# Query-block pipeline of both heads, and a top-k search in two alternating groups, in a two-layer decoder trunk

## The chip, the cores and the metric

The kernel runs on 1 core of a Trainium2 chip. The metric is device microseconds for one execution; the time of a kernel is the median of its runs. Engines are called PE (TensorE), DVE (VectorE), ACT (ScalarE), POOL (GpSimd) and SP (the engine whose queue issues the DMAs).

## What is computed

The reference is a trunk of two post-norm layers on x of 1024 tokens by 1024 features, float32. Each layer projects x once and feeds four groups of four heads; the group outputs are multiplied by a SiLU gate, projected back, added to x and normalised.

```python
def hybrid_layer(x, ...):
    p = split_columns(einsum("bsd,de->bse", x, w_in))
    ...
    for i in range(S // 128):                 # 8 query blocks, keys up to the block's end
        o_a = stick_breaking_block(...)       # sigmoid logits, reverse cumulative sum over keys
        o_b = diff_block(...)                 # two softmax maps, p0 - lam * p1, RMS norm per head
        o_c = dsa_block(...)                  # softmax over the 256 keys with the highest index scores
        o_d = mla_block(...)                  # low-rank attention with a rotary part
    y = concatenate(outs) * silu(p["gate"])
    return layer_norm(ALPHA * x + y @ w_out, ln_g, ln_b)
```

The index scores of group C are a weighted sum over 8 small heads of relu(q k); `top_k` takes 256 keys of each query.

## The kernel before, in words

**Work units.** A layer is walked in ten units (`ORDER`, line 42): s0 and s1 compute the index scores (`g_scores`), then a0, a1, d0, d1, b0, b1, c0, c1 are the attention groups, each unit two heads (`softmax_pair`, line 385). A unit goes over eight query blocks i; block i has n = 128(i+1) keys.

**Background.** Projections of the layer (`proj`, line 227: 24 matmuls of 512 columns into one bank, for two halves of the tokens), the low-rank chains of group D (`g_dkw` line 682, `g_dqw` line 718) and, from b1 on, half of the output projection (`g_out`, line 789) are generators in one list (`BGSEQ`). Each unit yields weights w, and `back.run(quota * w)` (line 1116) lets that much background be written between the unit's own steps. The order written is a priority: the instructions of each engine are put in their final order when the program is built, so in the trace the background stands between the attention's pieces, also where the program text has it elsewhere. Two calls shift that: `tc.high_priority(n)` and `tc.keep_in_program_order(ins)`.

**Steps of an attention unit** (`push`, line 363; loop at 498). For block i: stage 1 computes the scores of both heads into PSUM and the weights in SBUF; stage 2, once per head, transposes the weights by PE (`transposed`, line 344, line 95 in the trace: matmuls into a bank `trp`, then an ACT copy to `PT`, line 356); stage 3 multiplies by v (`pv`) and, every fourth block, calls `finalize` (line 323). `push` is called for each head: scores(i), background, transposes of (i-1, head 1), background, pv(i-1), transposes of (i, head 0), scores(i+1) and so on.

**Group A** (`stick`, line 392): each head's scores z take a buffer of their own of two PSUM banks (`sc`, 2 buffers). Four ACT operations (lines 403 to 406), a DVE scan (407), a DVE subtraction that reads z for the last time (408), and an ACT exponential (409). Groups B, C, D (`on_rows`, line 412): chunks of 512 keys; DVE copies each out with a running minimum (lines 436 and 438), ACT takes the exponential (442). Group B combines its two maps with line 465.

**PSUM.** `mm` has two banks, for projections; `tr` has one, `pv` one, `sc` two buffers of two banks. A transposed group of four blocks goes to `tr`, except in b0, b1, c0, c1 from the fifth key block on, where it goes to `mm` (line 349). SBUF tiles of the weights, of PT and of most background results share one pool of 8 (`wrk`, `N_P`).

**Top-k** (`g_topk`, line 855) is a generator of 24 steps, all on DVE: two counts over the six blocks 7 to 2, a maximum, 11 halvings of a threshold, three steps that find the eight largest values below the threshold (`below`, lines 911 to 914), six masks (`mask`, lines 946 to 951; the first with a few small operations and `ps_fail`), and a conditional that closes the search. A halving is

```python
counts(SB, t, cnt)          # six counting operations, line 874
nc.vector.scalar_tensor_tensor(neg, cnt, NSEL - 4.5, mx, op0=ALU.is_gt, op1=ALU.mult)
nc.vector.tensor_scalar(mx, mx, 0.5, None, op0=ALU.mult)
nc.vector.tensor_tensor(lo, lo, neg, op=ALU.add)
nc.vector.tensor_tensor(t, lo, mx, op=ALU.add)
```

The first count of each halving is kept in program order. `with_topk` (line 1072) pulls steps as a unit advances: 8 over a0, 10 over a1, 4 over d0, the rest in d1.

Of the kernel before, what the change touches and what calls it, by code (L numbers as in the profile page):

```python
# [41 lines left out]
ORDER = [('s0', 37.2, 0, 0.6), ('s1', 38.4, 0, 0.65), ('a0', 47.1, 8, 0.65), ('a1', 63.6, 10, 0.7), ('d0', 30.7, 4, 0.65), ('d1', 24.9, 4, 0.65), ('b0', 55.1, 0, 0.65), ('b1', 68.8, 0, 0.65), ('c0', 43.6, 0, 0.65), ('c1', 0.0, 0, 0.7)]  # L42
LNP = 1
TR_MM, PT_DVE = ('b0', 'b1', 'c0', 'c1'), ()
OUT_DVE = 1
PIN_A, PIN_S = 2, 0
OUT_AT = ('b1', 0.3)
FRAC, W0, W1 = 1, 2, 0.5
# [29 lines left out]


class Paced:  # L80


    def __init__(self, tc):
        self.tc, self.pin = tc, False

    def _issue(self, ins):
        if self.pin:
            self.tc.keep_in_program_order(ins)
        self.pin = False

    def matmul(self, *a, **k):
        self._issue(self.tc.nc.tensor.matmul(*a, **k))  # L92

    def transpose(self, *a, **k):
        self._issue(self.tc.nc.tensor.transpose(*a, **k))  # L95
# [3 lines left out]
def trunk(ctx: ExitStack, tc: tile.TileContext, t: dict, out: bass.AP, depth=DEPTH, dbg=None):  # L99
# [223 lines left out]
    def finalize(g, et, c, pv, gs, rl, subv):  # L323
        if g != 1:
            nc.vector.tensor_tensor(gs, pv, gs, op=ALU.mult)
            if g > 1:
                nc.vector.tensor_tensor(gs, rl, gs, op=ALU.mult)
        else:
            o = half("o_h")
            nc.scalar.activation(o, pv, AF.Copy)  # L330
            nc.vector.tensor_tensor(o, rl, o, op=ALU.mult)
            sq = half("sq_h")
            nc.scalar.activation(sq, o, AF.Square)
# [8 lines left out]
        nc.sync.dma_start(y_d[YPOS[et]][:, 512 * c:512 * c + 512], gs)  # L342

    def transposed(p, i, g, pair):
        nblk = i + 1
        pt = wrk([P, nblk, P], F32, "PT")
        for j0 in range(0, nblk, 4):
            m = min(4, nblk - j0)
            tr = mm_ps("trp") if j0 and f"{'abcd'[g]}{pair}" in TR_MM else tr_ps("trp")
            for j in range(m):  # L350
                te.transpose(tr[:, P * j:P * j + P], p[:, P * (j0 + j):P * (j0 + j) + P], ident)
            if j0 and f"{'abcd'[g]}{pair}" in PT_DVE:
                nc.vector.tensor_copy(pt[:, j0:j0 + m, :], tr[:, :P * m].rearrange("p (j n) -> p j n", j=m))
            else:
                with ahead(HP_T):
                    nc.scalar.activation(pt[:, j0:j0 + m, :], tr[:, :P * m].rearrange("p (j n) -> p j n", j=m), AF.Copy)  # L356
        return pt

    queue = []
    back = None  # L360
    te = Paced(tc)

    def push(w, pin, *stages):

        te.pin = pin & 1
        stages[0]()
        yield FRAC * w
        for it in list(queue):
            te.pin = pin & 2 if len(it) > 1 else pin & 4
            it.pop(0)()  # L370
            if not it:
                queue.remove(it)
        te.pin = False
        if len(stages) > 1:
            queue.append(list(stages[1:]))
        yield (1 - FRAC) * w

    def flush():
        while queue:
            for it in list(queue):  # L380
                it.pop(0)()
                if not it:
                    queue.remove(it)

    def softmax_pair(g, pair, scores, nmaps, nbt, scale, v, neglam=None, subv=None):
# [6 lines left out]
        def stick(i):  # L392

            n = P * (i + 1)
            z = {(h, 0): sc_ps("z") for h in range(2)}
# [3 lines left out]
            for h in range(2):  # L399
                zh = z[h, 0][:, :n]  # L400
                e, r = wrk([P, n], F32, "spe"), wrk([P, n], F32, "P0")
# [5 lines left out]
                nc.vector.tensor_tensor_scan(backwards(r, n), backwards(r, n), backwards(e, n), 0.0, ALU.add, ALU.add)  # L407
                nc.vector.tensor_tensor(r, zh, r, op=ALU.subtract)
                nc.scalar.activation(r, r, AF.Exp)
                st[i]["res", h] = [r]  # L410

        def on_rows(i):

# [3 lines left out]
            p = {hm: wrk([P, n], F32, f"P{hm[1]}") for hm in maps}  # L417
            mx = {hm: small([P, 3], F32, "mx") for hm in maps}
            low = {hm: 3e38 for hm in maps}
            far = env["ns"].get(i) if g == 2 else None  # L420
            used = 0
            for o in range(0, n, 512):
# [5 lines left out]
                for lo, hi in ((o, min(o + w, near)), (a, o + w)):  # L428
                    if lo >= hi:
                        continue  # L430
                    for h, m in maps:
                        out = mx[h, m][:, used:used + 1]
# [7 lines left out]
                    used += 1  # L440
            for h, m in maps:
                nc.scalar.activation(p[h, m], p[h, m], AF.Exp, bias=low[h, m], scale=-1.0,  # L442
                                     accum_out=st[i]["ls"][:, m, h, i % 4:i % 4 + 1])
            for h in range(2):
                st[i]["res", h] = [p[h, m] for m in range(nmaps)]

        def stage1(i, h):
            i4 = i % 4
            if i4 == 0 and h == 0:
                st["ls"] = small([P, nmaps, 2, 4], F32, "ls", tag="ls", bufs=2)  # L450
            if h == 0:
                st[i] = dict(ls=st["ls"], pts=[])
            if h == 0:
                (on_rows if g else stick)(i)

        def stage2(i, h):
# [14 lines left out]
            d["pts"].append(transposed(p, i, g, pair))  # L471

        def stage3(i, h):
            if h == 0:
                return
# [6 lines left out]
            for j in range(i + 1):  # L482
                for hh in range(2):
                    te.matmul(pv[64 * hh:64 * hh + 64, P * i4:P * i4 + P], v[j // 4][:, j % 4, vo + 64 * hh:vo + 64 * hh + 64],
# [4 lines left out]
            elif i4 == 3:  # L489

                rl = tr_ps("rl")
                for k in range(4):
                    for hh in range(2):
                        te.matmul(rl[64 * hh:64 * hh + 64, P * k:P * k + P],
# [3 lines left out]
        for i in range(NB):  # L498
            for h in range(2):
                yield from push((i + W0) / (16 * W0 + 56), PIN_S, lambda: stage1(i, h), lambda i=i, h=h: stage2(i, h),  # L500
                                lambda i=i, h=h: stage3(i, h))
# [9 lines left out]
    for l in range(depth):  # L511
# [343 lines left out]
        def g_topk():  # L855
# [9 lines left out]
            blocks = (7, 6, 5, 4, 3, 2)  # L865
# [33 lines left out]
            for _ in range(HALVES):  # L899
                counts(SB, t, cnt)  # L900
                nc.vector.scalar_tensor_tensor(neg, cnt, NSEL - 4.5, mx, op0=ALU.is_gt, op1=ALU.mult)
                nc.vector.tensor_scalar(mx, mx, 0.5, None, op0=ALU.mult)
                nc.vector.tensor_tensor(lo, lo, neg, op=ALU.add)
                nc.vector.tensor_tensor(t, lo, mx, op=ALU.add)
                yield

# [109 lines left out]
        def products(ps, maps, ops, i, o, w, rows_of, first=True, last=True):  # L1016

            qh, ql, kh, kl = ops
            for k, (x, y) in enumerate(((qh, kh), (ql, kh), (qh, kl))):
                for hm in maps:  # L1020
                    r = rows_of(*hm)
                    te.matmul(ps[hm][:, :w], x[r, P * i:P * i + P], y[r, o:o + w], start=first and k == 0,
                              stop=last and k == 2, tile_position=(r.start, 0))

        def score_a(pair):
            def f(ps, maps, i, o, w, near):
                tail = o + w == P * (i + 1)
                products(ps, maps, env[f"a{pair}t"], i, o, w, lambda h, m: slice(64 * h, 64 * h + 64), last=not tail)
                if tail:
                    for hm in maps:  # L1030
                        te.matmul(ps[hm][:, w - P:w], u_b, id_b, start=False, stop=True)
# [7 lines left out]
        def score_c(pair):  # L1039
            def f(ps, maps, i, o, w, near):  # L1040
# [3 lines left out]
                if msk:  # L1044
                    for hm in maps:
                        te.matmul(ps[hm][:, a - o:w], id_b, ns[i][:, a:o + w], start=False, stop=True)
# [253 lines left out]
```

## Time and profile before

| what | value |
|---|---|
| median of 3 runs (lowest, highest) | 1829.26 us (1827.39, 1833.37) |
| the profiled execution's own time | 1826.64 us |
| its span, first to last instruction | 1824.8 us |
| PE busy | 1680.8 us, 92% of the span |
| DVE, ACT, POOL busy | 63%, 47%, 24% |
| mean granted PE clock | 0.966 of full speed |

How to read it: the sums of the prediction are made against the profiled execution, whose time is 1.84 us more than its span. Busy time of PE counts matmuls that overlap as one stretch; its idle time is what no matmul covers. A row of the waits names who waited, on which line, for what.

### The profile page before, as it was taken

To read this page: it belongs to the slowest core of one execution; us is meant where nothing else is said; L and a number is where in the kernel's file an instruction comes from. 1 tells how busy PE (TensorE), PEld (TensorE's weight loads), DVE (VectorE), ACT (ScalarE), POOL (GpSimd) and SP (SyncE) were. 2 spreads that over 40 slices of the span, in tenths; PEclk is the share of its full clock that TensorE was granted. 3 is DMA by queue.
4 is the path that set the end of the run, shared out by engine and by line. 5 is a ranking of instruction groups with operands and counts; after the bars stand their busy time and mean duration, and the time that the engine had idled before them with its cause. 6 is when DMAs were issued, how large, how long until landed. Compare 5 with 4: busy or idle time off the path is not lost. (4 is left out here: it accounts for less than half of the span.)

```text
span 1824.8 us, 29123 instructions
## 1 busy us (share of the span) xinstructions
PE 1680.8 (92%) x10886; PEld 1246.0 (68%) x10886; DVE 1155.1 (63%) x2605; ACT 860.9 (47%) x1715; POOL 445.8 (24%) x406
## 2 busy tenths in 40 slices
PE   7998888899999999899999997989999999988997
PEld 5686666677676776576777765757776767765775
DVE  5777788865346445454866778898553555554448
ACT  3436757533355443345434466574334454433452
POOL 4232123422122312110322321233212222212012
PEclk9999979999999999899999998999999999998999
DMA  6221122525223236544331211235242322565343
GB/s 190 76 90 39 35 96 76 186 84 162 105 77 109 81 118 217 165 152 138 141 90 39 95 35 48 83 118 191 64 145 93 110 93 76 165 197 163 111 145 110
DMA packets 117034, 205.70 MB, mean 113 GB/s; under 512 B 11113, under 2 KB 41369, under 8 KB 116889
## 3 DMA queue, kind: packets, MB, share of 16 engines
q1 hardware_dynamic: 116888, 203.81, 33.9%
q8 instruction: 86, 1.41, 0.3%
q14 instruction: 60, 0.48, 0.1%
HBM read 131.92 MB, written 71.32 MB: 111 GB/s over the span
## 5 line engine op out<-in xcount | busy, mean ns | idle before, releaser
L236 PE MATMUL ps_pj<-xh,whi 128*128 128x512 f32 x832 | 349.2, 420 | 13.0 <-ACT xh L527 9.9
L197 POOL TENSOR_SCALAR whi<-wraw 128x512 fp32r<-128x512 f32 (+1 forms) x154 | 114.8, 746 | 923.1 <-PE ps_pj L236 573.8
L236 PE MATMUL ps_pj<-xl,whi 128*128 128x512 f32 x832 | 335.6, 403 | 0.4 <-DVE xl L528 0.4
L236 PE MATMUL ps_pj<-xh,wlo 128*128 128x512 f32 x832 | 334.7, 402 | 0.0
L356 ACT ACTIVATE PT<-trp 128x512 f32<-128x512 f32 (+3 forms) x384 | 182.0, 486 | 314.5 <-PE trp L95 307.6
L442 ACT ACTIVATE P<-P,mx 128x128 f32<-128x128 f32 (+7 forms) x256 | 195.9, 767 | 137.8 <-DVE mx L436 63.1
L95 PE MATMUL trp<-ident,P 128*128 128x128 f32 x1152 | 198.5, 287 | 32.9 <-ACT PT L356 12.0
L198 POOL TENSOR_TENSOR wlo<-wraw,whi 128x512 fp32r<-128x512 f32 (+1 forms) x154 | 216.0, 1403 | 14.0 <-PE ps_pj L236 1.4
L95 PEld LDWEIGHTS trp<-ident,P 128*128 128x128 f32 x1152 | 131.4, 142 | 101.1 <-ACT PT L356 33.4
L236 PEld LDWEIGHTS ps_pj<-xh,whi 128*128 128x128 f32 x832 | 160.2, 192 | 56.8 <-issue 23.1
L92 PE MATMUL pv<-PT,v 128*64 128x128 f32 x2304 | 190.1, 284 | 3.2 <-ACT PT L356 3.0
L236 PEld LDWEIGHTS ps_pj<-xh,wlo 128*128 128x128 f32 x832 | 159.6, 192 | 36.7 <-issue 2.6
L236 PEld LDWEIGHTS ps_pj<-xl,whi 128*128 128x128 f32 x832 | 160.7, 193 | 33.4 <-issue 5.2
L92 PEld LDWEIGHTS pv<-PT,v 128*64 128x64 f32 x2304 | 137.6, 138 | 60.0 <-issue 43.8
L438 DVE TENSOR_SCALAR_CACHE_REDUCE P<-ps_r 128x512 f32<-128x512 f32 (+3 forms) x160 | 83.4, 567 | 139.8 <-PE ps_r L92 120.2
L92 PE MATMUL ps_r<-op 64*128 64x512 f32 (+7 forms) x1152 | 156.5, 389 | 3.7 <-DVE P L438 3.0
L849 DVE SCALAR_TENSOR_TENSOR S<-rel,iw,S 128x512 f32<-128x512 f32 (+3 forms) x140 | 109.9, 787 | 36.4 <-ACT rel L843 30.6
L874 DVE TENSOR_SCALAR_CACHE_REDUCE junk<-S,t 128x1024 bf16<-128x1024 f32 (+1 forms) x132 | 124.2, 941 | 2.9
L407 DVE TENSOR_TENSOR_SCAN P<-P,spe 128x128 f32<-128x128 f32 (+7 forms) x64 | 91.8, 1435 | 43.3 <-ACT spe L406 43.3
L92 PEld LDWEIGHTS ps_r<-op 32*128 32x128 f32 (+1 forms) x1152 | 81.5, 184 | 55.1 <-issue 34.6
L258 PE MATMUL ps_v<-whi,xh 128*128 128x256 f32 x384 | 112.6, 294 | 0.3 <-DVE kl L296 0.3
L258 PE MATMUL ps_v<-wlo,xh 128*128 128x256 f32 x384 | 110.3, 288 | 0.0
(231 smaller groups left out, 2866.3 us busy)
## 6 DMA issues: line engine op xcount, KB each, us to landing
wraw<-in_wqk_dram SPq DMA_DIRECT2D x104, 256.0 KB, 2.6
g_d<-gate SPq DMA_DIRECT2D x32, 256.0 KB, 2.0
gs_h<-g_d SPq DMA_DIRECT2D x32, 256.0 KB, 3.7
y_d<-gs_h SPq DMA_DIRECT2D x32, 256.0 KB, 2.1
yraw<-y_d SPq DMA_DIRECT2D x32, 256.0 KB, 3.4
part_d<-xo SPq DMA_DIRECT2D x32, 256.0 KB, 2.7
tt<-part_d SPq DMA_DIRECT2D x16, 512.0 KB, 6.5
wraw<-in_wv_dram SPq DMA_DIRECT2D x24, 256.0 KB, 3.0
```

Of the source, the lines that this page charges most:

```text
L92: self._issue(self.tc.nc.tensor.matmul(*a, **k))
L95: self._issue(self.tc.nc.tensor.transpose(*a, **k))
L197: nc.gpsimd.tensor_scalar(hi, raw, 1.0, 0.0, op0=ALU.mult, op1=ALU.add)
L198: nc.gpsimd.tensor_tensor(lo, raw, fb(hi), op=ALU.subtract)
L236: nc.tensor.matmul(ps, a[:, k4, :], b[:, kb, 512 * c:512 * c + 512], start=(n == 0), stop=(n == 23))
L258: nc.tensor.matmul(pv, a[:, kb, P * sb:P * sb + P], b[:, k2, :], start=(n == 0), stop=(n == 23))
L356: nc.scalar.activation(pt[:, j0:j0 + m, :], tr[:, :P * m].rearrange("p (j n) -> p j n", j=m), AF.Copy)
L407: nc.vector.tensor_tensor_scan(backwards(r, n), backwards(r, n), backwards(e, n), 0.0, ALU.add, ALU.add)
L438: nc.vector.tensor_scalar(dst, src, -scale, low[h, m], op0=ALU.mult, op1=ALU.min, accum_out=out)
L442: nc.scalar.activation(p[h, m], p[h, m], AF.Exp, bias=low[h, m], scale=-1.0, accum_out=st[i]["ls"][:, m, h, i % 4:i % 4 + 1])
L849: nc.vector.scalar_tensor_tensor(s[:, o:o + w], r[:, h, :w], sc, s[:, o:o + w], op0=ALU.mult, op1=ALU.add)
L874: ins = nc.vector.tensor_scalar(junk[:, :P * (i + 1)], arr[i], th, None, op0=op, op1=ALU.add, accum_out=dst[:, k:k + 1])
```

## The change

An attention unit makes one step per query block instead of two. `step` writes the scores of block i and the transposes of both heads of block i-1 alternately, then yields one weight w (one stretch of background instead of two half as long), then writes pv(i-1). For group B the scores come in chunks of 512 keys, with a head's transposes after each chunk. The end of `finalize` for group B (`norm`) is held over to the next step. Transposed groups take `tr` and `mm` by turns, in all units. In `stick`, blocks of up to 512 keys put both heads in one `sc` buffer and run the ACT operations and the subtraction once for both heads. The top-k's blocks are (7, 4, 2) and (6, 5, 3): each halving counts one group and then the other, and a group's threshold is updated between the counts of the other. Steps are pulled as 7 over a0, 7 over a1, 5 over d0, 4 over d1 and 1 over b0.

```diff
-ORDER = [..., ('a0', 47.1, 8, 0.65), ('a1', 63.6, 10, 0.7), ('d0', 30.7, 4, 0.65), ('d1', 24.9, 4, 0.65), ('b0', 55.1, 0, 0.65), ...]
+ORDER = [..., ('a0', 47.1, 7, 0.65), ('a1', 63.6, 7, 0.7), ('d0', 30.7, 5, 0.65), ('d1', 24.9, 4, 0.65), ('b0', 55.1, 1, 0.65), ...]
...
     def finalize(g, et, c, pv, gs, rl, subv):
+        def out():
+            nc.sync.dma_start(y_d[YPOS[et]][:, 512 * c:512 * c + 512], gs)
+
...
+        def norm():
             ms = tr_ps("ms_b")
             for h in range(2):
                 r = slice(64 * h, 64 * h + 64)
-                te.matmul(ms[r], on256[r, :64], sq[r], start=True, stop=True)
+                nc.tensor.matmul(ms[r], on256[r, :64], sq[r], start=True, stop=True)
...
+            out()
+
+        pipe["late"].append(norm)
...
-            tr = mm_ps("trp") if j0 and f"{'abcd'[g]}{pair}" in TR_MM else tr_ps("trp")
+            tr = (mm_ps if k + j0 // 4 & 1 else tr_ps)("trp")
...
+    def step(w, scores, turn, values):
+
+
+        old = pipe["turn"], pipe["values"]
+        for k in range(max(len(scores), len(old[0]))):
+            for stage in (scores, old[0]):
+                if k < len(stage):
+                    stage[k]()
+        yield w
+        after(old[1])
+        pipe.update(turn=turn, values=values)
+
+    def after(values):
+        late, pipe["late"] = pipe["late"], []
+        for f in late + values:
+            f()
...
-            z = {(h, 0): sc_ps("z") for h in range(2)}
+            if n <= 512:
+                zs = [sc_ps("z").rearrange("p (h n) -> p h n", h=2)[:, :, :n]]
+                z = {(h, 0): zs[0][:, h] for h in range(2)}
+            else:
+                zs = [sc_ps("z").unsqueeze(1)[:, :, :n] for _ in range(2)]
+                z = {(h, 0): zs[h][:, 0] for h in range(2)}
...
+            chunks = [lambda k=k, o=o: chunk(k, o) for k, o in enumerate(range(0, n, 512))]
+            return chunks if nmaps > 1 else [lambda: [f() for f in chunks]]
...
-            for h in range(2):
-                yield from push((i + W0) / (16 * W0 + 56), PIN_S, lambda: stage1(i, h), lambda i=i, h=h: stage2(i, h),
-                                lambda i=i, h=h: stage3(i, h))
+            yield from step((i + W0) / (8 * W0 + 28), stage1(i), [lambda i=i, h=h: stage2(i, h) for h in range(2)],
+                            [lambda i=i: stage3(i)])
...
-            blocks = (7, 6, 5, 4, 3, 2)
+            blocks = (7, 4, 2, 6, 5, 3)
...
+            for it in range(HALVES):
+                for g in range(2):
+                    (q, bl), other = half3[g], half3[1 - g][0]
+                    count(q, bl, 0)
+                    if it or g:
+                        compare(other)
+                    nc.vector.scalar_tensor_tensor(q["base"], q["mx"], -0.5, q["t"], op0=ALU.mult, op1=ALU.add)
+                    count(q, bl, 1)
+                    if it or g:
+                        advance(other)
+                    count(q, bl, 2)
                 yield
```

`count` is one counting operation, kept in program order for the first block of a group; `compare` is one small DVE operation and `advance` two, on tiles of 128 by 3. The class `Paced` goes away; its pin was always 0 in the attention's matmuls.

## Rows read from the trace of the kernel before

**Rows 1.** The page: the span, and the engines' busy time.

```profile
span 1824.8 us, 29123 instructions
PE 1680.8 (92%) x10886; PEld 1246.0 (68%) x10886; DVE 1155.1 (63%) x2605; ACT 860.9 (47%) x1715; POOL 445.8 (24%) x406
```

**Rows 2.** Busy time by stretch: a0, a1, d of layer 0; a0, a1, d of layer 1.

```profile
core 0: us, PE busy (x) PEld busy (x) DVE busy (x) ACT busy (x) POOL busy (x), PEclk, DMA share, GB/s
...
141.00:240.00 99.00, 83.70 (x441) 60.27 (x441) 77.76 (x134) 67.03 (x122) 21.26 (x19) 0.88 0.10 31
240.00:372.00 132.00, 113.86 (x659) 85.54 (x658) 115.45 (x206) 79.54 (x146) 41.27 (x38) 0.95 0.40 131
372.00:490.00 118.00, 116.90 (x888) 87.30 (x889) 65.35 (x146) 45.13 (x105) 25.94 (x22) 0.99 0.32 107
...
1039.00:1137.00 98.00, 82.75 (x437) 59.60 (x438) 76.77 (x133) 66.01 (x122) 21.31 (x19) 0.88 0.09 30
1137.00:1269.00 132.00, 115.38 (x660) 87.19 (x660) 114.82 (x206) 80.23 (x146) 43.13 (x38) 0.93 0.40 131
```

**Rows 3.** PE's waits, whole span: waiting tile and line, released by; us, times, longest.

```profile
PE z L92 <- DVE P L408: 21.2, 18, 2.6
PE trp L95 <- ACT PT L356: 12.0, 18, 2.1
...
PE ps_kn L664 <- DVE kn L694: 9.9, 2, 4.9
...
PE ms_b L92 <- ACT sq_h L333: 6.4, 8, 1.5
...
PE ps_dq L664 <- DVE dqo L739: 5.5, 4, 2.3
PE trp L95 <- ACT cqrs L655: 5.2, 2, 3.2
PE trp L95 <- ACT sq_h L338: 3.3, 6, 0.8
```

**Rows 4.** Timeline: start us, us, engine, line; [idle before <- releaser]. DVE's queue in a0.

```profile
223.23 1.28 DVE L874 TENSOR_SCALAR_CACHE_REDUCE junk<-S,t 128x1024 bf16<-128x1024 f32 x1
...
228.40 0.69 DVE L694 TENSOR_TENSOR kn<-ps_kn,ckvrs 128x512 f32<-128x512 f32 x1
```

**Rows 5.** The same timeline, PE: the matmul behind it, and z of a1's first block.

```profile
229.14 1.22 PE L664 MATMUL ps_kn<-ckv,whi 128*128 128x512 f32 x2 [4.95 <-DVE kn L694]
...
235.72 0.44 PE L92 MATMUL z<-kh,qh 64*128 64x128 f32 x1 [2.50 <-DVE P L408]
...
239.17 0.44 PE L92 MATMUL z<-kh,qh 64*128 64x128 f32 x1 [2.36 <-DVE P L408]
```

**Rows 6.** Busy time by stretch, 25 us windows around a0's end, columns as in Rows 2.

```profile
225.00:250.00 25.00, 13.95 (x67) 10.74 (x68) 23.60 (x44) 13.15 (x22) 3.04 (x1) 0.59 0.29 101
...
1125.00:1150.00 25.00, 16.32 (x79) 12.50 (x80) 23.62 (x44) 12.09 (x21) 4.96 (x3) 0.60 0.35 128
```

**Rows 7.** Line 902, whole span: ns min/median/max; then its busy us and count.

```profile
L902 DVE TENSOR_SCALAR mx<-mx x22: 157/172/1190, 203.4 to 1241.6; 128x6 f32<-128x6 f32 x22
...
0.00:1825.00 1825.00, 6.25 (x22) 0.97 0.34 113
```

**Rows 8.** Line 913 by the same view; the first and last of five operations of mask 7.

```profile
0.00:1825.00 1825.00, 10.65 (x12) 0.97 0.34 113
...
377.32 0.75 DVE L946 TENSOR_SCALAR eq<-S,t 128x1024 f32<-128x1024 f32 x1
...
383.20 0.43 DVE L951 TENSOR_SCALAR ky<-ky 128x1024 bf16<-128x1024 bf16 x1
```

**Rows 9.** PE timeline, a0's fourth block: the first product of each head.

```profile
160.40 0.50 PE L92 MATMUL z<-kh,qh 64*128 64x512 f32 x1 [0.76 <-DVE P L408]
...
162.72 0.50 PE L92 MATMUL z<-kh,qh 64*128 64x512 f32 x1
```

**Rows 10.** Groups of instructions: the copies of four transposed blocks, whole span.

```profile
L356 ACT ACTIVATE PT<-trp 128x512 f32<-128x512 f32 x192 | 112.0, 592 | 177.4 <-PE trp L95 171.2 <-issue 2.9 <-DMA dq_d<-hl 2.6
```

More of the change, by code (lines that the diff above doesn't have):

```diff
@@ L348, in transposed @@
             m = min(4, nblk - j0)
-            tr = mm_ps("trp") if j0 and f"{'abcd'[g]}{pair}" in TR_MM else tr_ps("trp")
+            tr = (mm_ps if k + j0 // 4 & 1 else tr_ps)("trp")
             for j in range(m):
[L351 to L356, printed above, removed]
+                nc.tensor.transpose(tr[:, P * j:P * j + P], p[:, P * (j0 + j):P * (j0 + j) + P], ident)
+            with ahead(HP_T):
+                nc.scalar.activation(pt[:, j0:j0 + m, :], tr[:, :P * m].rearrange("p (j n) -> p j n", j=m), AF.Copy)
         return pt
-    queue = []
     back = None
[L361 to L376, printed above, removed]
-    def flush():
[L379 to L383, printed above, removed]
+    pipe = dict(turn=[], values=[], late=[])
+    def step(w, scores, turn, values):
[11 more added lines that the diff above has]
+            f()
+    def flush():
+        for f in pipe["turn"]:
+            f()
+        after(pipe["values"])
+        after([])
+        pipe.update(turn=[], values=[])
     def softmax_pair(g, pair, scores, nmaps, nbt, scale, v, neglam=None, subv=None):
@@ L427, in on_rows @@
                 scores(ps, maps, i, o, w, near)
[L428 removed]
+                for q, (lo, hi) in enumerate(((o, min(o + w, near)), (a, o + w))):
                     if lo >= hi:
@@ L898, in g_topk, with count, compare, advance @@
             yield
[L899 to L904, printed above, removed]
+            half3 = []
+            for g in range(2):
+                k3 = slice(3 * g, 3 * g + 3)
+                q = {nm: sm(f"{nm}{g}", shape=[P, 3]) for nm in ("t", "mx", "cnt", "base", "hit")}
+                nc.vector.tensor_copy(q["t"], t[:, k3])
+                nc.vector.tensor_copy(q["mx"], mx[:, k3])
+                half3.append((q, blocks[k3]))
+            def count(q, bl, k):
+                n = P * (bl[k] + 1)
+                ins = nc.vector.tensor_scalar(junk[:, :n], SB[bl[k]], q["t"][:, k:k + 1], None, op0=ALU.is_gt, op1=ALU.add,
+                                              accum_out=q["cnt"][:, k:k + 1])
+                if k == 0:
+                    tc.keep_in_program_order(ins)
+            def compare(q):
+                nc.vector.scalar_tensor_tensor(q["hit"], q["cnt"], NSEL - 4.5, q["mx"], op0=ALU.is_gt, op1=ALU.mult)
+            def advance(q):
+                nc.vector.tensor_tensor(q["t"], q["base"], q["hit"], op=ALU.add)
+                nc.vector.tensor_scalar(q["mx"], q["mx"], 0.5, None, op0=ALU.mult)
+            for it in range(HALVES):
+                for g in range(2):
+                    (q, bl), other = half3[g], half3[1 - g][0]
[7 more added lines that the diff above has]
+                    count(q, bl, 2)
                 yield
+            compare(half3[1][0])
+            advance(half3[1][0])
+            for g in range(2):
+                nc.vector.tensor_copy(t[:, 3 * g:3 * g + 3], half3[g][0]["t"])
             m8, oh = sm("m8", shape=[P, nb, 8]), sm("oh", shape=[P, nb, 8])
@@ L1021, in products @@
                     r = rows_of(*hm)
-                    te.matmul(ps[hm][:, :w], x[r, P * i:P * i + P], y[r, o:o + w], start=first and k == 0,
+                    nc.tensor.matmul(ps[hm][:, :w], x[r, P * i:P * i + P], y[r, o:o + w], start=first and k == 0,
                               stop=last and k == 2, tile_position=(r.start, 0))
```

100 lines of the change are left out of this document (42 added, 58 removed).

## The prediction

> **What bounds the kernel now.** I read the page first: PE is busy for 1680.8 us of a span of 1824.8, so all that an unchanged amount of matmul work can give back is some 144 us of idle time, and what the lower clock costs [rows 1]. Next, busy time by stretch says where that idle time lies. In a0 and a1 PE is idle for 99 - 83.7 = 15.3 and 132 - 113.9 = 18.1 us in layer 0, and for 15.3 and 16.6 in layer 1: 65.3 us in all. There DVE is the fullest of the other engines (77.8 of 99 and 115.5 of 132 us), and the granted clock is down to 0.88 and 0.93 to 0.95 [rows 2]. In d, right behind, PE is idle for 1.1 of 118 us, and DVE is busy for only 65.4 [rows 2]. So group A with the top-k beside it is held by DVE, and the rest by PE. Third, PE's waits name the releasers: 21.2 us for the subtraction of line 408, which frees the scores' buffer, 9.9 and 5.5 us for background results of DVE (kn, dqo), 12.0 and 5.2 us at a transpose whose bank is still being read, and in group B 6.4 and 3.3 us around the RMS norm [rows 3]. Last, the timeline shows one such wait from inside: a count of 1024 starts at 223.23, the counts of the other blocks stand behind it in DVE's queue, kn comes only at 228.40 [rows 4], and the matmul that needs its bank has then been idle for 4.95 us [rows 5].
>
> The end of a0 is the dearest place: the clock averages 0.59 and 0.60 over 25 us in the two layers [rows 6]. Of two levels, full and half, that is some 20 us at 1.2 GHz; the stretch of idle PE before it is the one just told.
>
> **The change, part by part** (sums over both layers, against the profiled execution's 1826.6 us; the median of the runs shown is 2.6 us above it).
>
> *DVE work in a0 and a1.* Before, steps 1 to 18 of the top-k are pulled there, after, 1 to 14. What leaves is the three `below` steps and mask 7. Line 913 takes 10.65 us in the trace; 911 and 914, of the same shapes, are taken as equal, so 32 us in both layers. Mask 7 runs from 377.32 to 383.6, 6.3 us per layer [rows 8]. Together 32 + 12.6 = 44.6 us, 22.3 per layer. What comes is small operations: a halving has 4 before and 8 after (per group one compare, one base, two in advance), so 4 x 11 = 44 more per layer, and 6 copies. The nearest row is line 902: 0.172 us at the median, 1.19 at most, 6.25 / 22 = 0.284 on average [rows 7]. At the average 50 x 0.284 = 14.2 us per layer (at the median 8.6). DVE in a0 and a1 thus gets 22.3 - 14.2 = 8.1 us per layer lighter, out of 77.8 + 115.5 = 193. That is 4%, far less than the list of steps suggests. That the average is above the median is work of POOL: it is busy for 62.5 of 231 us in a0 and a1 [rows 2], and a small operation now and then lasts as long as one of POOL's.
>
> The Trainium skill has a rule for this (SBUF — State Buffer, Who interferes with whom): a DVE instruction with two SBUF inputs, or in a two-port mode, and a GpSimd instruction that reads SBUF exclude each other for the whole instruction. By it the added operations, not the counts, are the ones that get stuck; the trace agrees, with 1.19 us where 0.17 is usual [rows 7].
>
> *What that gives PE.* The waits that DVE can shorten are 21.2 + 9.9 + 5.5 = 36.6 us [rows 3]; the bounds are 0 (the load hardly falls) and all of them. Two mechanisms are visible. A burst between two pinned places is now three counts instead of six, so a background result waits for half a burst: half of 15.4, say 8 us. And where both heads of a short block share a buffer, head 1 of a1's first block no longer waits for the second buffer: that wait was 2.36 us [rows 5], once per layer, with parts of others some 6 us. I take 14.
>
> *Scores of group A.* In blocks 1 to 4 the two heads' products can now run side by side. In the fourth block of a0 they stand 2.3 us apart [rows 9]. The first product of the fourth block lasts 0.50 us [rows 9], a head has three, and the blocks before it are a quarter, a half and three quarters as wide: 3 x 0.50 x 2.5 = 3.75 us per unit if all of head 1's products were hidden, 15 us in four units, and nothing if they stand together already. I take 3, near the low end, since a matmul's busy time overlaps that of the next, and only the streaming is saved. The merged ACT operations cost nothing and gain nothing: ACT is busy for 67 of 99 us there [rows 2], and head 0's scan now starts one half-width later, under the longer background stretch.
>
> *Clock.* In the two low stretches PE is busy for 13.95 and 16.3 us [rows 6], four fifths of it at half speed, which costs about 12 us. Bounds 0 and 12; a third is taken, 4, as the cause gets shorter but stays.
>
> *Two banks for transposes.* The 12.0 + 5.2 us at the `tr` bank [rows 3]: bounds 0 and 17, half is taken, 8. The counterpart is the mm bank. Before, in b and c, blocks 5 to 8 send one group per head there: 8 per unit, 4 units, 2 layers, 64. After, it is 12 per unit in 8 units, 192: 128 more. Each holds one of the projections' two banks for four transposes and a copy of 0.592 us [rows 10], a good microsecond. Where the projection's other bank is being filled, which takes 24 matmuls, it costs nothing; where it is full and being read, PE loses what is left of the hold. Bounds 0 and 128 x 1 us. I take 0.06 us each, 8 us, near the low end, since in b and c, where it is done already, only 12.0 us of transposes wait for a copy at all [rows 3].
>
> *Held-over norm of group B.* 6.4 + 3.3 us [rows 3] were PE standing at the norm's matmul and at the bank that its result held. A block later the operands are long there: 8 of the 9.7. Its output DMA moves back one step in SP's queue; weight loads behind it then wait less. Its data is needed only at the layer's end.
>
> *d and b.* d takes over 22.3 us per layer, and its DVE goes from 65.4 to some 88 of 118 [rows 2]: cover enough, but a score buffer comes free later now and then; 0 to 10 us, 3 taken. The closing conditional moves from d1 to b0, the same instructions: nothing, as DVE waits for it in either place. In b the four weight tiles of block i are claimed before those of i-1 are transposed, so all 8 tiles of the pool can be in use and a projection's result waits for a slot; 0 to 12 us, 4 taken.
>
> *Sum:* -14 - 3 - 4 - 8 + 8 - 8 + 3 + 4 = -22 us: 1826.6 - 22 = 1804.6 for a profiled execution, 1807 for the median.
>
> **The rivals.**
> - *Much faster.* The longer single stretch of background per block covers the chain of group A, DVE never runs late, and the clock holds. Then 36.6 + 3 + 12 + 17.2 + 9.7 = 78 us are the ceiling; two thirds, 50 us, give 1779. For it: the waits are few and long, and sit at places that the change touches. Against it: DVE's load falls by only 4%.
> - *No change.* DVE stays the bound of a0 and a1, halvings and all, the small operations eat what the moved steps free (at 0.4 us each, 50 cost 20), and the mm bank eats the rest: 1824 to 1834.
> - *Slower: the mm bank.* Transposes of A and D hold one of two banks while ACT is at a chain of block i+1 that stands ahead of the copy. The projections, which fill PE in exactly these units, then run on one bank. Without the mm term the sum is -30 us, so it decides from 30 / 128 = 0.23 us per added group; at 0.4 us the kernel is 51 - 30 = 21 us slower, 1850. For it: the copy waits behind up to eight ACT operations of a block in a0, a1; against it: the copies may go first, where they are ready first.
> - *It does not do what it says.* The order of each engine is set when the program is built, and a different text may give much the same order; this falls into no change.
>
> **How the numbers follow.** A measurement of this kernel tells about 0.3%, 5.5 us, from no change. The forecast has 0.49, much faster 0.14, no change (with the text that does nothing) 0.15, slower 0.22. So faster by over 0.3% 0.63, within it 0.15, slower 0.22. The range goes from 1777, a little below the faster rival, to 1843, in the slower rival's lower half (the point of 0.34 us per group); it leaves out some 0.07 below and 0.12 above. The forecast's own range is 1790 to 1823.
>
> **What would show it.** Right: PE idle in a0 and a1 falls from 65 us to some 45; the clock at a0's end is above 0.8; the waits at ms_b are gone; the transposes' waits for the copies fall from 12 to some 6; small operations by the hundred with 0.25 to 0.3 us each; DVE in d near 88 of 118. Wrong: rows in which ps_pj waits for PT's copy (the mm bank), or for a slot of the pool in b; line 407 or 408 as late as before with DVE at 90%; a new low clock stretch in a1, whose halvings now go on to its end.

## The result and the profile after

The changed kernel takes **2019.8 us** (median of 4 runs, 2014.7 to 2028.7) against 1828.3 us before (4 runs): a ratio of 1.105, with a 95% interval of 1.100 to 1.109. Forecast were 1807, and 1843 at most. The page of the profiled execution (2014.7 us), its first lines, answers to [rows 1]:

```profile
span 2012.9 us, 29113 instructions
PE 1769.7 (88%) x10886; PEld 1318.0 (65%) x10886; DVE 1159.6 (58%) x2689; ACT 850.1 (42%) x1635; POOL 430.5 (21%) x406
```

The span is 188.1 us longer. The number of matmuls is the same (10886), and yet PE is busy for 88.9 us more; the other 99.2 us are idle time of PE. DVE and ACT are busy as long as before within 11 us, in a longer span. So no engine got more to do: PE waits more, and between its waits it runs more slowly (mean granted clock 0.918, before 0.966).

To see where, the busy time by stretch, cut where the last results of a1, of d1, of b1 and of c1 are scaled by DVE in layer 0 (columns as in [rows 2]). First the kernel before, at these cuts, then the changed one:

```profile
141.00:391.00 250.00, 216.34 (x1259) 161.71 (x1259) 205.19 (x371) 151.29 (x278) 62.53 (x57) 0.92 0.27 88
391.00:528.00 137.00, 133.66 (x997) 97.11 (x999) 63.39 (x148) 59.31 (x135) 32.25 (x28) 1.00 0.31 105
528.00:765.00 237.00, 221.77 (x1498) 164.66 (x1494) 126.91 (x411) 99.65 (x222) 56.68 (x52) 0.99 0.41 136
765.00:865.00 100.00, 95.81 (x722) 66.17 (x722) 47.17 (x167) 51.41 (x119) 11.24 (x14) 0.97 0.44 144
```

```profile
141.00:410.00 269.00, 219.08 (x1197) 165.27 (x1198) 186.57 (x372) 146.83 (x238) 60.71 (x57) 0.85 0.26 85
410.00:559.00 149.00, 144.56 (x1063) 107.80 (x1061) 85.94 (x187) 57.23 (x135) 30.73 (x28) 0.98 0.26 90
559.00:865.00 306.00, 260.36 (x1491) 191.11 (x1487) 125.80 (x418) 102.31 (x226) 52.21 (x52) 0.87 0.31 105
865.00:964.00 99.00, 92.52 (x719) 64.68 (x719) 46.66 (x164) 49.86 (x115) 11.26 (x14) 0.98 0.46 149
```

Group B, which the prediction looked at last, lost most: 237 to 306 us, of which 30 are idle time of PE (15.2 to 45.6 us) and 39 are busy time, at a granted clock of 0.87 in place of 0.99. Group A lost 19 (idle 33.7 to 49.9, clock 0.92 to 0.85), D 12, and C nothing. Layer 1 repeats the pattern (B takes 303 us there, before 238).

The waits of PE over the whole span answer to [rows 3] (the columns are the same):

```profile
PE trp L338 <- ACT PT L340: 59.9, 23, 5.9
PE z L1046 <- DVE P L400: 33.5, 8, 11.6
PE ps_r L1046 <- DVE cf L458: 28.8, 6, 7.5
PE trp L338 <- DVE P L460: 17.8, 30, 1.2
PE ps_r L1046 <- DVE P L433: 16.5, 12, 2.5
PE ps_r L1046 <- DVE mx L431: 14.6, 18, 2.1
```

In the changed kernel line 338 is a transpose, 340 the copy to PT, 393 to 401 the chain of group A (399 the scan, 400 the subtraction), 431 and 433 the copies of scores by DVE, 458 to 460 the combination of B's maps, and 1046 the score matmuls. Of the first row 50.9 us lie in group A and 8.0 in D; the second is group A's. Before, these rows had 12.0 us, of which 4.6 in A, and 21.2 us. The others belong to group B, but for 0.8 us; of them the kernel before has the fourth, with 6.5 us (its line 465), and the fifth, with 3.0 (its line 438). Blocks are counted from 0 here.

**Group A, from inside.** The timeline in a0, PE and then ACT (start, length, engine, line; idle before and its releaser):

```profile
194.48 0.71 PE L338 MATMUL trp<-ident,P 128*128 128x128 f32 x5
...
200.27 0.47 PE L338 MATMUL trp<-ident,P 128*128 128x128 f32 x1 [3.68 <-ACT PT L340]
```

```profile
194.63 0.81 ACT L393 ACTIVATE spe<-z 128x768 f32<-128x768 f32 x1 [6.26 <-PE z L1055]
195.34 0.80 ACT L394 ACTIVATE P<-z 128x768 f32<-128x768 f32 x1
...
198.87 0.86 ACT L395 ACTIVATE spe<-spe 128x768 f32<-128x768 f32 x1
199.60 0.62 ACT L340 ACTIVATE PT<-trp 128x512 f32<-128x512 f32 x1
```

The scores of block 5 are written ahead of the transposes of block 4, so their chain is ahead in ACT's queue: seven operations of 0.8 us. The first transposes are done by 195.2, their copy begins at 199.60, and PE, which needs the bank for the next ones, has nothing to do for 3.68 us. There are eight such waits in group A of layer 0, 5.9 us at most.

Here ACT was at work all the time. In the longest wait of z, which comes in both layers, it was not:

```profile
169.25 1.04 PE L338 MATMUL trp<-ident,P 128*128 128x128 f32 x8
...
184.66 0.79 PE L1046 MATMUL z<-kh,qh 64*128 64x512 f32 x1 [11.59 <-DVE P L400]
```

```profile
171.79 0.75 ACT L396 ACTIVATE spe<-spe 128x640 f32<-128x640 f32 x1
...
184.63 0.74 ACT L401 ACTIVATE P<-P 128x640 f32<-128x640 f32 x1 [9.77 <-DVE P L400]
185.28 1.06 ACT L340 ACTIVATE PT<-trp 128x512 f32<-128x512 f32 x2
```

```profile
182.19 1.49 DVE L399 TENSOR_TENSOR_SCAN P<-P,spe 128x640 f32<-128x640 f32 x1
```

The input of block 4's first scan is there at 172.5, but counts of the top-k fill DVE until 182.2. ACT's exponential (401) stands 9.77 us for the subtraction behind the scan; the copies of block 3, whose transposes were done at 170.3, come only after it, at 185.28; and PE waits 11.59 us for the score buffer. So these two waits, one in each layer, make up 23 of the 33.5 us in the row of z, and the top-k has a part in them. The page Perfetto Trace Analysis of the Trainium skill (Tensor Engine Instruction) says that ACT and DVE take their instructions strictly first in, first out; the trace agrees: the copies, ready at 170.3, waited behind an operation that was not.

**Group B, from inside.** The timeline in b1, DVE and then PE:

```profile
757.29 0.56 DVE L433 TENSOR_SCALAR_CACHE_REDUCE P<-ps_r 128x384 f32<-128x384 f32 x1 [10.23 <-DMA cv_d<-v]
```

```profile
750.80 0.28 PE L238 MATMUL ps_v<-wlo,xh 128*128 128x256 f32 x1
758.55 1.48 PE L1046 MATMUL ps_r<-op 32*128 32x512 f32 x3 [7.47 <-DVE cf L458]
```

DVE is to copy block 4's scores to its fourth weight tile, and all 8 tiles of the pool are taken: four by block 3's weights, which are not transposed yet, three by block 4's, and one by a projection's result until the DMA to `cv_d` has left it. DVE's queue stands for 10.23 us, the score buffers stay full, and PE waits for 7.47 us. The row names `cf`, the last DVE operation before PE goes on; the copies that free the buffers stand right ahead of it. Over the span DVE's waits of this kind are

```profile
DVE P L433 <- PE pv L477: 38.9, 8, 9.5
DVE P L433 <- DMA cv_d<-v: 29.3, 4, 10.3
DVE P L433 <- DMA g_d<-gate: 15.7, 6, 5.5
DVE P L433 <- DMA b1k_d<-hl: 9.8, 4, 3.0
```

The last three, 54.8 us, are tiles that a DMA has to leave. The first I read as tiles of PT that wait for pv, since with ten tiles (e4) it is gone like the others. It costs PE less than its length: pv stands behind the background, and in the one that ends at 744.68 PE is busy with that. Before, DVE has no such row for a DMA, and 5.0 us for pv.

### The profile page after: what moved, and what is told of

It reads as the page before. It is cut to its first block, busy times and chain, and to the rows that moved or that the text cites. A ratio compares the mean times of both kernels' runs of the same rounds, so it can differ in the third digit from the quotient of the medians.

```text
span 2012.9 us, 29113 instructions
## 1 busy us (share of the span) xinstructions
PE 1769.7 (88%) x10886; PEld 1318.0 (65%) x10886; DVE 1159.6 (58%) x2689; ACT 850.1 (42%) x1635; POOL 430.5 (21%) x406
## 5 line engine op out<-in xcount | busy, mean ns | idle before, releaser
L177 POOL TENSOR_SCALAR whi<-wraw 128x512 fp32r<-128x512 f32 (+1 forms) x154 | 106.5, 692 | 1061.4 <-PE ps_pj L216 625.3
L340 ACT ACTIVATE PT<-trp 128x512 f32<-128x512 f32 (+3 forms) x384 | 175.4, 486 | 293.1 <-PE trp L338 271.3
L338 PE MATMUL trp<-ident,P 128*128 128x128 f32 x1152 | 204.2, 311 | 84.5 <-ACT PT L340 59.9
L1046 PE MATMUL ps_r<-op 64*128 64x512 f32 (+7 forms) x1152 | 184.7, 411 | 61.8 <-DVE cf L458 28.8
L338 PEld LDWEIGHTS trp<-ident,P 128*128 128x128 f32 x1152 | 144.4, 157 | 135.7 <-ACT PT L340 83.1
L477 PE MATMUL pv<-PT,v 128*64 128x128 f32 x2304 | 204.8, 290 | 15.6 <-ACT PT L340 12.7
L178 POOL TENSOR_TENSOR wlo<-wraw,whi 128x512 fp32r<-128x512 f32 (+1 forms) x154 | 208.0, 1351 | 23.6 <-PE ps_pj L216 11.8
L477 PEld LDWEIGHTS pv<-PT,v 128*64 128x64 f32 x2304 | 144.9, 141 | 86.9 <-issue 48.8
L1046 PEld LDWEIGHTS ps_r<-op 32*128 32x128 f32 (+1 forms) x1152 | 96.1, 197 | 121.4 <-issue 70.9
L238 PE MATMUL ps_v<-whi,xl 128*128 128x256 f32 x384 | 114.2, 298 | 0.0
```

What stands on the lines that cost most here:

```text
L177: nc.gpsimd.tensor_scalar(hi, raw, 1.0, 0.0, op0=ALU.mult, op1=ALU.add)
L178: nc.gpsimd.tensor_tensor(lo, raw, fb(hi), op=ALU.subtract)
L238: nc.tensor.matmul(pv, a[:, kb, P * sb:P * sb + P], b[:, k2, :], start=(n == 0), stop=(n == 23))
L338: nc.tensor.transpose(tr[:, P * j:P * j + P], p[:, P * (j0 + j):P * (j0 + j) + P], ident)
L477: nc.tensor.matmul(pv[64 * hh:64 * hh + 64, P * i4:P * i4 + P], v[j // 4][:, j % 4, vo + 64 * hh:vo + 64 * hh + 64], pts[hh][:, j, :], sta ...
L1046: nc.tensor.matmul(ps[hm][:, :w], x[r, P * i:P * i + P], y[r, o:o + w], start=first and k == 0, stop=last and k == 2, tile_position=(r.sta ...
```

## The experiments

Theory 1 puts the whole loss down to the order inside `step`: scores of block i stand ahead of the transposes of block i-1. Rivals were the new top-k, the banks, the size of the pool and a copy's place in ACT's queue. The kernel before ran beside each set, and ratios are to these runs: 11 times for e9 to e12 (median 1831.3 us), and once each for e1 to e4 (1834.4), e5 to e8 (1827.9) and e13 to e15 (1841.4), which were run once themselves. These three differ by 0.7%, so a ratio from single executions is not known better than that.

**e1: the old step, the rest new.** The loop over `push` with its half-steps and the norm at once come back; top-k, banks and side-by-side scores stay as changed.

```diff
...
+            sc = stage1(i)
+            for h in range(2):
+                yield from push((i + W0) / (16 * W0 + 56), lambda: [f() for f in sc] if h == 0 else None, lambda i=i, h=h: stage2(i, h),
+                                lambda i=i, h=h: stage3(i) if h else None)
```

> The changed kernel with the old pipeline of half steps (scores, half the background, transposes of the other head, half the background, values, transposes of head 0) and the norm at once; top-k, banks and shared score buffers as changed. Theory 1 (the step's order is the cause: scores are written ahead of the transposes of the block before, so weight tiles are claimed too early and copies stand behind the next block's chain): about 1830 us, and b back to some 275 us per layer from 340. Theory 2 (the top-k's place and order are the cause): hardly better than 2010, a0 still 20 us longer. Theory 3 (transposes in the mm banks): hardly better than 2000.

1824.8 us, where the kernel before took 1834.4: the loss is gone with the step, while top-k, banks and score buffers are still the changed ones. B takes 237 us in layer 0.

**e2: the old top-k in the changed kernel** (the halving, its block order and the steps per unit).

```diff
-            blocks = (7, 4, 2, 6, 5, 3)
+            blocks = (7, 6, 5, 4, 3, 2)
...
+            for _ in range(HALVES):
+                counts(SB, t, cnt)
```

> The changed kernel with the top-k as before (six counts in a row, four small operations, steps pulled 8, 10, 4, 4); all else as changed. Theory 1: about 2000 us, b as long as in the changed kernel. Theory 2: about 1850. A part of both: a0's stretch shortens by some 20 us per layer, the total falls by 40 to about 1975.

2007.3 us (0.094 above before): the top-k is not the cause of most of it. The transposes' waits for PT are still 50.3 us; those of z fall from 33.5 to 22.2.

**e3: transposes first.** All else as changed.

```diff
-        for k in range(max(len(scores), len(old[0]))):
-            for stage in (scores, old[0]):
-                if k < len(stage):
-                    stage[k]()
+        for stage in old[0] + scores:
+            stage()
```

> The changed kernel with one thing turned round: in a step, the transposes of block i-1 are all written ahead of the scores of block i. Theory 1: the copies stand ahead of the next chain and the weight tiles of i-1 are free before those of i are claimed, so about 1840 to 1880 us, and the waits of line 433 for DMAs of background tiles go away. Theory 2 and 3: within 20 us of 2015.

1780.9 us: better than both kernels, with these two lines alone, and by more than the 1840 to 1880 that I expected. The waits of line 433 for DMAs are gone.

**e4: ten tiles in place of eight,** in the changed order.

```diff
-N_B, N_P, N_H, N_W, N_R, N_S = 17, 8, 4, 4, 2, 10
+N_B, N_P, N_H, N_W, N_R, N_S = 15, 10, 4, 4, 2, 10
```

> The changed kernel with 10 tiles instead of 8 in the pool that weights, transposed weights and background results share, and 15 instead of 17 in the pool of operands. If the shared pool is what makes b long: b shortens by 40 us or more per layer, total about 1900 to 1930, and line 433's waits for cv_d, g_d and b1k_d, 55 us in the changed kernel, fall below 10. If only the order of the copies counts: within 20 us of 2015. Fewer operand tiles may cost some 10 us at unit ends.

1966.2 us. Between the same two operations as in the tables B takes 276 us in layer 0 (567 to 843), 30 less than in the changed kernel, where I had expected 40 or more, and the total lies between my two figures. Of the three rows of 54.8 us 0.5 is left; a new one, line 431 for `c0q_d`, has 11.4. So the pool is a part of B's loss, somewhat under half, and not of A's: the waits for PT are 58.4 us.

**e5: PT's copies with a higher priority,** `HP_T` = 100 in place of 0.

> The changed kernel with the copies of transposed blocks (line 340) put 100 places ahead in priority; the transposes and scores are written in the changed order. If the copies behind the next block's chain are the cause in a and d: PE's waits for them fall from 60 to under 20 us and the total by 30 to 60, to about 1960 to 1985; b, whose loss is the tiles, stays some 300 us per layer. If where the copies stand does not matter: within 20 us of 2015.

1975.5 us, inside the range of the first theory, and B takes 305 us as it said, but the sign it went by fails: the transposes' waits for PT fall only from 59.9 to 56.3. So the total came out by luck. What fell is the waits of z, from 33.5 to 16.5, as the one of 11.6 us is gone, and those of pv for PT, from 12.7 to 1.6; A is 14 us shorter in layer 0 (142 to 397). Why the priority does not carry the copies past the chain was not tested.

**e6: transposes first in group B alone** (`first` is nmaps > 1).

```diff
+        if first:
+            for stage in old[0] + scores:
+                stage()
+        else:
...
```

> The changed kernel with the transposes written ahead of the scores in b0 and b1 only; a, c and d keep the changed order. If b and the others lose by causes of their own, this gives b's share: b back to some 226 us per layer from 306, so 160 us less, about 1860, and a as long as in the changed kernel (141 to 282 for a0). If the late copies of a are what delays b as well: above 1950.

1873.1 us, a ratio of 1.025. B takes 232 us, so some 0.08 of the 0.105 lies in B, and PE's waits for PT and for z are as in the changed kernel (62.1 and 33.3 us).

**e7 and e8: what the other parts are worth in the good order.** e3 with the old top-k, and e3 with the old rule for the banks.

> The kernel with the transposes ahead everywhere (1781 us), and the top-k as before. If the new top-k is worth what was forecast: some 10 to 20 us slower, 1790 to 1800. If its small operations cost as much as it frees: within 6 us. If the spread is what made 1781 possible: 1810 or more.

> The kernel with the transposes ahead everywhere (1781 us), and the old rule for the banks of transposed groups (mm only in b and c, from the fifth key block on). If two banks by turns help, as forecast with 8 against 8 us: within 10 us of 1781. If sharing the projections' banks costs: 1760 or less. If the second bank is what the new order lives on, as both heads' groups come in a row: 1800 or more.

```diff
-            tr = (mm_ps if k + j0 // 4 & 1 else tr_ps)("trp")
+            tr = (mm_ps if j0 and mm else tr_ps)("trp")
```

1814.8 us (ratio 0.993) and 1833.6 us (1.003), each from one execution. Against e9 below (0.975) the new top-k is worth 0.0175, some 32 us, and the banks by turns 0.028, some 51 us. e8's loss lies, in layer 0 and at the same cuts, in A (237 us in e9, 246 in e8) and D (143 and 154), which by the old rule have one bank for all transposes, more than in B (226 and 230).

**e9: e3's order, run six times.**

> The order of e3 again (all transposes of block i-1 ahead of the scores of block i), timed in rounds. Theory 1 (the order inside the step is the whole loss, and the other parts of the change are a gain): 1775 to 1787 us, ratio to the kernel before 0.970 to 0.976. Rival (the 1780.9 of e3 was one lucky execution, and the parts left over are worth nothing): the ratio is 0.99 or more.

Ratio 0.975 (0.972 to 0.978), 1786.1 us beside 1831.3: some 45 us faster than the kernel before. Its stretches, to be read against the two tables above:

```profile
141.00:378.00 237.00, 205.68 (x1192) 156.31 (x1192) 180.99 (x372) 148.03 (x239) 64.21 (x57) 0.91 0.30 97
378.00:521.00 143.00, 141.16 (x1072) 106.00 (x1072) 87.80 (x194) 59.42 (x135) 32.47 (x28) 1.00 0.28 93
521.00:747.00 226.00, 219.78 (x1483) 164.97 (x1479) 129.81 (x409) 99.18 (x222) 54.42 (x52) 0.99 0.44 143
747.00:845.00 98.00, 91.69 (x728) 63.26 (x729) 47.49 (x167) 51.87 (x119) 11.55 (x14) 1.00 0.46 147
```

In B PE is idle for 6.2 us, less than half of the 15.2 before; D takes 6 us longer with DVE at 87.8, as work came there from A. The order has a price of its own: the transposes now wait 18.4 us for the last exponential of A (line 399 there), 1.0 in the changed kernel.

**e10: turns kept, the transposes first at each.** Transposes of head 0, scores of chunk 0, transposes of head 1, scores of chunk 1.

```diff
-            for stage in (scores, old[0]):
+            for stage in (old[0], scores):
```

> The turn-taking of scores and transposes stays, but at each turn the transposes come first: transposes of head 0, scores of chunk 0, transposes of head 1, scores of chunk 1. Theory 1a (what costs is that even the first transposes, and so the first PT copy, stand behind scores): most of the loss goes, 1790 to 1830 us. Theory 1b (what costs is any chain of ACT, and any claim of weight tiles, between the transposes of one block's two heads): the second head's PT copies still stand behind the chain, and the second head's tiles of block i-1 are still held while those of block i are claimed; 1880 to 1980 us, and the waits of the transposes for the PT copy stay above 25 us.

Ratio 1.019 (1.015 to 1.023), 1862.6 us: between my two figures. A is nearly mended (it ends at 389 instead of 410, in e9 at 378), B is not (259 us; 226 in e9). The transposes' waits for PT are 3.8 us, so the sign of theory 1b, over 25, fails. In the kernel before and in e1 the transposes of head 1 stand behind the next block's scores too, but with half of the background in between; e10 has none written there. What that half is worth was not measured.

**e11: e9 with the norm made at once. e12: e9 with a score buffer for each head of A.**

```diff
-        pipe["late"].append(norm)
+        norm()
```

> The order of e3 with the norm made at once instead of held over to the next block's values. By the prediction's term (held-over norm, 8 us): 1785 to 1793 us, and TensorE's waits of ms_b for sq_h are back at about 6 us. Rival (in the good order the wait is hidden, since the next block's work is queued otherwise): within 3 us of the order of e3.

> The order of e3, but each head of the stick-breaking scores has a score buffer of its own also where the block has 512 columns or fewer, so that |z|, relu, exp and ln run once for each head again. By the prediction's term (scores of A side by side, 3 us): 1782 to 1788 us. Rival (one buffer for both heads makes the first scan wait for both heads' chain, and costs as much as it saves): within 2 us of the order of e3 or faster.

e11: 0.982 (0.979 to 0.985), 1800.0 us; the held-over norm is worth 14 us, more than the waits for it, which are 1.4 us (ms_b) and 3.3 us (the transpose behind it) in this run. e12: 0.976 (0.973 to 0.980), 1790.5 us; not told apart from e9.

**e13: in group A, the chain alone moved.** e6, with the scores of A still ahead of the old transposes on PE, and the chain of block i (`last`) behind them.

```diff
+            return lambda: chain(i, n, zs)
+
+        def chain(i, n, zs):
             for k, zh in enumerate(zs):
...
+        last()
         yield w
         after(old[1])
```

> The kernel of e6 (transposes first in b alone, 1873 us) with one more edit, in group A: the scores of block i still stand ahead of the transposes of block i-1 on TensorE, but the chain of block i (ACT's abs, relu, exp, ln, DVE's scan and subtraction, ACT's exp) is written behind the transposes of block i-1 and their PT copies. Theory 1 (in group A it is the PT copies behind the next block's chain of ACT that cost): units a0 and a1 come back to nearly what they are in the order of e3, so 1805 to 1835 us, and the transposes' waits for the PT copy fall from 62 us to 20 or less. Rival (it is the order on TensorE, scores ahead of transposes, that costs, since the scores wait for a buffer that the last block's subtraction frees): 1860 us or more, with the waits of z as in e6, 33 us.

1809.0 us beside 1841.4, ratio 0.982, in place of e6's 1.025. PE's waits, whole span:

```profile
PE z L1054 <- DVE P L408: 22.2, 14, 3.3
...
PE trp L338 <- ACT PT L340: 14.0, 12, 3.7
```

Down from 33.3 and 62.1 us. So in A it is not the order on PE that costs, but the chain ahead of the copies of PT. a1 ends at 381, where it was 410. The edit moves DVE's part of the chain and its claims of tiles as well; the claims are not it (e4), and ACT's part and DVE's were not told apart.

**e14: e10 with ten tiles. e15: e9 with ten tiles.**

> The order of e10 (transposes first at each turn, 1862.6 us) with ten weight tiles instead of eight. Theory 1 (in e10 group A and D are mended, and b still claims four tiles while the second head's two of the block before are held): the pool makes up a third to two thirds of what e10 loses to e9 (76 us), 1810 to 1838 us. Rival (the second head's PT copies behind the first chain are the whole remainder): within 10 us of e10, 1852 to 1872 us.

> The order of e3 with ten weight tiles instead of eight. Theory 1 (the pool binds in the changed kernel only because of the order: two or three blocks' tiles are not held at once any more): within 8 us of the order of e3, 1778 to 1794 us. Rival (eight tiles are too few in any order): faster by 10 us or more, below 1776 us.

e14: 1875.8 beside 1841.4, ratio 1.019, as e10. My theory for it falls: B takes 254 us, 5 less than in e10, so once the transposes of head 0 go first the pool hardly binds, and what B still loses is something else. (A ends at 406 where e10 had 389. In e4 and e15, which also have two tiles fewer in the pool of operands, it ends later too: 417 for 410, and 389 for 378. That pool was not tested by itself.) PE's waits in B, by releasers of which e9 has no row over 0.5 us there (e14, from 549 to 803):

```profile
PE trp L338 <- DVE P L460: 7.2, 11, 1.5
...
PE ps_r L1046 <- DVE P L433: 4.0, 4, 2.2
PE ps_r L1046 <- DVE mx L431: 1.6, 2, 1.2
```

Head 1's combination (line 460) stands in DVE's queue behind the copies of the next block's first scores, which wait for PE, and head 1's transposes wait for it. That reading of the rows was not tested by itself. e15: 1801.3 us, outside my range, but the kernel before took 1841.4 beside it: the ratio is 0.978, within the interval of e9. B takes 227 us (532 to 759), in e9 226: in the good order two more tiles gain nothing there.

## Why the prediction was wrong

**The step that failed** is the price of writing the scores of block i ahead of the transposes of block i-1. Its only term was the pool in b: "In b the four weight tiles of block i are claimed before those of i-1 are transposed, so all 8 tiles of the pool can be in use and a projection's result waits for a slot; 0 to 12 us, 4 taken." The mechanism was there, and the term was sized at less than a tenth. Measured, in layer 0: 30 us go when the pool has ten tiles (e4), and 80 when the order is turned (306 to 226, e9). Rows with a wait for a slot in b stand among the prediction's signs of being wrong, and they came. Two things were missed. The slot is waited for by DVE, not by the background: its copy of scores stands at the head of its queue, so the score buffers and with them PE stop too. And what was claimed too early was one sign of a wider fault, that work which can go stands, on DVE and ACT, behind work which cannot. That the order is the cause in B is shown (e6, e9); how what the pool does not explain divides among the waits there is not.

**The same fault in A** was put at nothing. "Two banks for transposes" took half of 17.2 us as a gain (-8) with a cost of 8 at the mm bank. With the chain ahead of the copies two banks did not keep the waits down: a copy that starts 4.4 us late (195.2 to 199.60) leaves its bank that much later. The waits rose from 12.0 to 59.9 us (e13: back to 14.0). The prediction saw these copies, but only in the rival on the mm bank, and let them delay the projections. That rival named "a chain of block i+1 that stands ahead of the copy", had the sign right, and missed the victim: ps_pj waits for PT for 0.5 us in the whole span. It was the transposes themselves that stood. Its price of 0.4 us per group came to 1850.

**The clock** was counted as a gain of 4 us. The waits just told come with PE busy for 88.9 us more on the same matmuls, nearly half of the loss. No term had asked what new idle time would cost beside its own length.

**The other terms,** in the order where they can be seen (e9):
- DVE waits of A: -14, with -4 for the clock and +3 in d; measured by e7, -32 for the new top-k as a whole (one execution). With the old top-k PE is idle in A for 44.3 us (257 less 212.7), with the new for 31.3. DVE in A has 181.0 us of work in layer 0, against 205.2 before, three times the relief that the prediction took; and DVE in d is at 87.8, where "near 88" was forecast (of 118 us; it is 143).
- Small operations: 0.25 to 0.3 us each were forecast. The four kinds of the changed kernel (lines 908, 911, 912, 920) sum to 12.59 + 8.46 + 8.14 + 8.98 = 38.17 us for 176, 0.217 each.
- Two banks: -8 + 8 = 0; measured -51 (e8, one execution). With all transposes of a block in one piece and one bank, they wait 16.9 us for PT, with two 4.6; no wait at the mm bank shows in e9. That is the smaller part: of the 47.8 us between the two spans 12.9 are idle time of PE and 34.9 busy time at the same mean clock (0.967 and 0.968), 24.0 of it in the transposes, and why is open. The prediction also misread its row: the 12.0 us are the whole span's, and b and c have only 1.4 of them.
- Held-over norm: -8; measured -14 (e11). ms_b's wait is gone, as forecast.
- Side-by-side scores: -3; measured -4 (e12), not told from nothing.
- PE's idle time in a0 and a1 was to fall from 65 to 45: it rose, to some 50 in layer 0 alone, and is 31.3 there in e9, against 33.7.

These gains sum to 32 + 51 + 14 + 4 = 101 us, of which e9 shows 45. They were taken away one at a time from the kernel that has all of them, and the step by whole blocks may need the banks more than the old one did; what that step costs by itself was not measured. So the parts with a forecast gain went that way where they could be told from nothing, and by more; the order that carried them lost 234 us (2019.8 less 1786.1).

## What to carry to other kernels

When a pipeline over blocks puts the next block's first stage ahead of the last block's second, ask on every engine, not only PE, what ready work now stands behind work that is not, and which pool's slots are claimed before the old ones are given back. A claim that has to wait holds up everything behind it on the engine that makes it (DVE for 10.23 us above), and what fills that engine's inputs is next (PE for 7.47). Write the stage that frees buffers first and the one that claims them last: here two lines in place of four made 1.105 into 0.975.

## What the hardware showed that was not expected

Short, repeated waits came with about as much loss again as their own length: PE is idle for 99.2 us more, and busy for 88.9 us more on the same matmuls. In the stretch of B (559 to 865) the granted clock is 0.87, and PE was idle for 45.6 of 306 us, with 7.5 us as its longest wait; before, with 15.2 of 237 us idle, it was 0.99. Around two of the stops it is lower still:

```profile
728.00:738.00 10.00, 5.61 (x25) 5.04 (x26) 3.54 (x15) 2.55 (x7) 0.00 (x0) 0.70 0.27 105
748.00:760.00 12.00, 4.53 (x30) 3.51 (x28) 2.67 (x15) 2.33 (x6) 7.52 (x8) 0.83 0.41 129
```

By these two rows PE does nothing for 4.4 of 10 and 7.5 of 12 us. What that does to work that waits for nothing shows behind the first of these stops, which ends at 732.18. PE is busy without a gap with the same background matmuls, first at the lower of the clock's two levels (0.50, 1.2 GHz), then at the higher (1.00, 2.4 GHz):

```profile
735.00:738.50 3.50, 3.50 (x18) 3.50 (x18) 0.33 (x2) 0.25 (x1) 0.00 (x0) 0.50 0.00 0
739.00:742.00 3.00, 3.00 (x27) 3.00 (x27) 0.00 (x0) 0.00 (x0) 0.00 (x0) 1.00 0.03 5
```

That is 18 matmuls in 3.5 us and 27 in 3.0.

A term for a new wait on PE is therefore not done with the length of the wait.
